# GpSimd's low parts of weights: operations of 256 columns in place of 512

## The chip, the cores and the metric

The kernel runs on one core of a Trainium2 chip. The metric is the device time of one execution in microseconds (us). The engines are TensorE (PE; PEld is its loading of weights), VectorE (DVE), ScalarE (ACT), GpSimd (POOL) and SyncE (SP, which issues nearly all the transfers). Line numbers such as L197 are those of the kernel before; the change adds four lines, so that L197 there reads L201 in the changed kernel, and L186 reads L188.

## What is computed

One inference step of a two-layer decoder trunk, for a prompt of 1024 positions and for 8 sampled sequences of 8 positions each, with one set of float32 weights. Layer 0 mixes tokens by a gated depthwise convolution beside a stick-breaking attention, layer 1 by a short gated convolution beside a causal pooling. Each mixer has an input and an output projection, and each layer ends in a SwiGLU block. Cut to what matters here:

```
def swiglu(h, w_in, w_out):
    g, u = jnp.split(h @ w_in, 2, axis=-1)
    return (jax.nn.silu(g) * u) @ w_out

    for layer in range(DEPTH):
        hn = rms_norm(h, norm_mix_g[layer])
        mix = ...            # projections hn @ w_in, token mixer, @ w_out
        h = h + mix
        h = h + swiglu(rms_norm(h, norm_ffn_g[layer]), w_ffn_in[layer], w_ffn_out[layer])
    y = rms_norm(h, norm_final_g)
```

D_MODEL is 1024 and FFN_DIM is 2816, so that nearly all of the arithmetic is products of activations with weight matrices of 1024 rows or columns.

## The kernel before, in words

**Tokens.** The 1088 columns (1024 of the prompt, 64 sampled) are worked in two groups: GA has columns 0 to 511, GB columns 512 to 1087 (576 of them, in two pieces of 288). Activations lie with channels on partitions.

**Products in three passes.** A float32 operand is split into a high part, which is the operand rounded to the format that PE multiplies (`fp32r`), and a low part, the remainder. A product is three matmuls: high weight by high activation, high by low, and low weight by high activation (`mm3`, L231 to L236; L235 is the matmul).

**Weights.** Weight blocks of 128 by 1024 values are loaded by SP into `stage` (4 buffers). `w_split` (L175) makes from each an `hl` tile (3 buffers): ACT writes the high part, POOL the low part as `stage - high`. The list `seq` fixes the order, and `w_next` (L222) hands out the next `hl` and first has the splits up to two blocks further on issued. For a **plain** block (L183 to L187) ACT writes all 1024 columns in one operation (L184), and POOL subtracts in two operations of 512 columns (L186). The weights of the output projection of the SwiGLU block are such plain blocks too.

**Forms.** Most of the SwiGLU input projections are done by a scheme with 7 products in place of 8 (`strassen`, L504; its matmuls are L511). For each pair of weight blocks, gate `sg` and up `su`, it needs sums of their halves: DVE makes them (L200, L201, L202, and L214 for the last), and `cut` (L194) splits each of the 7 halves of 512 columns: ACT writes the high part (L196), POOL the low part in one operation of 512 columns (L197). They go into four `hl` tiles, r = 0 to 3, with 2, 2, 2 and 1 halves. The 7 products use them in that order; the last product needs r = 3, which is the sum `sum_c`. DVE adds the products together from PSUM (L515), ACT applies the activation (L540), and POOL multiplies the two halves of the SwiGLU (L490); the result `hid` is split by ACT (L240) and DVE (L241).

**Order.** The kernel is scheduled by hand: every engine runs its instructions in the order in which the Python code issues them. In the SwiGLU block two `strassen` calls are followed by two output blocks (`run_ffn`, L544 to L580), in which DVE adds each result to `hb` (L295); the sums for the next `strassen` are put between these adds (L576). In `strassen`, the fourth accumulator W waits until DVE has emptied the first one. Other work of POOL lies between the low parts: squares (L252), products (L490, L465), and in layer 1 some splits of activations (L1755).

Of the kernel before, what the change touches and what calls it, by code (L numbers as in the profile page):

```python
# [12 lines left out]
OP = mybir.AluOpType  # L13
# [16 lines left out]
def f32(ap):  # L30
    return ap.bitcast(F)
# [26 lines left out]
def trunk_kernel(ctx, tc, x_prompt, x_sample, cache_k, cache_v, state_conformer, state_shortconv, state_pool,  # L58
# [4 lines left out]
    pe, act, dve, pool, sp = nc.tensor, nc.scalar, nc.vector, nc.gpsimd, nc.sync  # L63
# [97 lines left out]
    def w_load(upto):  # L161
        while nxt[0] < min(upto, len(loads)) and nxt[0] - 4 not in stage:
            i = nxt[0]
            src, kt = loads[i]
            stage[i] = wpool.tile([128, 1024], F, name="stage", bufs=4)
            sp.dma_start(stage[i].rearrange("p (k n) -> p k n", k=kt), src)
            nxt[0] += 1

    def need(upto):
        a, b, _ = seq[min(upto, len(seq)) - 1]  # L170
        return max(a, b or 0) + 1

    sums, parts_, thin = {}, [], [False]

    def w_split(upto):  # L175
        while nxt[1] < min(upto, len(seq)):
            i = nxt[1]
            a, b, r = seq[i]
            w_load(need(i + 1))
            hl = wpool.tile([128, 2, 1024], FR, name="hl", bufs=3)  # L180
            lo, hi = slice(0, 512), slice(512, 1024)
            if b is None:
                st = stage.pop(a)  # L183
                act.activation(hl[:, 0], st, AF.Copy)  # L184
                for c in (lo, hi):
                    pool.tensor_tensor(hl[:, 1, c], st[:, c], f32(hl[:, 0, c]), op=OP.subtract)  # L186
                hls[i] = hl.rearrange("p s (k n) -> p s k n", k=loads[a][1])  # L187
            else:  # L188
                sg, su = stage.get(a), stage.get(b)
                if r == 0:  # L190
                    sums["a"], sums["b"] = (sums["p"].tile([128, n], F, name=f"sum{n}") for n in (1024, 512))
                sa, sb = sums["a"], sums["b"]

                def cut(hl=hl, src=None):  # L194
                    for c, x in zip((lo, hi), src):
                        act.activation(hl[:, 0, c], x, AF.Copy)  # L196
                        pool.tensor_tensor(hl[:, 1, c], x, f32(hl[:, 0, c]), op=OP.subtract)  # L197

                if r == 0:
                    todo = [lambda: dve.tensor_tensor(sb, su[:, lo], su[:, hi], op=OP.add),  # L200
                            lambda: dve.tensor_tensor(sa[:, hi], sg[:, lo], su[:, lo], op=OP.subtract),  # L201
                            lambda cut=cut: (dve.tensor_tensor(sa[:, lo], sb, sg[:, lo], op=OP.subtract),  # L202
                                     cut(src=(sa[:, lo], sa[:, hi])))]
                    if thin[0]:
                        parts_.extend(todo)
                    else:
                        for f in todo:
                            f()
                else:
                    while parts_:  # L210
                        parts_.pop(0)()
                    if r == 2:
                        sums["c"] = sums["p"].tile([128, 512], F, name="sum_c")
                        dve.tensor_tensor(sums["c"], sg[:, hi], sa[:, lo], op=OP.subtract)  # L214
                    cut(src=(sb, sg[:, lo]) if r == 1 else (su[:, hi], sg[:, hi]) if r == 2 else (sums["c"],))
                if r == 2:
                    stage.pop(a), stage.pop(b)
                hls[i] = hl.rearrange("p s (f k n) -> p s f k n", f=2, k=4)
            nxt[1] += 1
    wj = [0]  # L220

    def w_next(live=0):  # L222
        j = wj[0]
        wj[0] += 1
        w_split(j + 3 - live)
        w_load(need(j + 6 - live))
        return hls.pop(j)
# [155 lines left out]
    def run_out(g, accs, x, gcol, ks=K0, slot=lambda: None, then=None):  # L383
        then = then or (g, x)

        def fin(n, a):
            added(g, hb[:, n, g.cs], a)
            add_squares(g, hb[:, n, g.cs], n == 0)

        a0, a1 = pair(g, accs, x, ks, {}, slot)  # L390
        fin(0, a0)
        fin(1, a1)
        for n in range(2, 6):
            slot()
            h = w_next()
            a = accs()
            block(g, a, h, x, ks, slot=slot)
            fin(n, a)
        slot()
        a0, a1 = pair(g, accs, x, K0, {k: [lambda k=k: prep(*then, k, pc(gcol + k)), lambda: low(0)]  # L400
                                       for k in range(6)}, slot)
        w_split(wj[0] + 3)
        for n, a in ((6, a0), (7, a1)):
            fin(n, a)
            prep(*then, n, pc(gcol + n))
            low(1)
        low()
# [290 lines left out]

    feed(GA, x1a, 0)
    w_split(2)  # L700
    feed(GA, x1a, 1)
    feed(GA, x1a, 2)
# [1240 lines left out]
```

## Time and profile before

| | |
|---|---|
| median of 3 runs | 2638.32 us (2637.15 to 2640.58) |
| time of the profiled execution | 2634.16 us |
| its span, first to last instruction | 2632.3 us |
| DVE busy | 1665.4 us (63%), 2330 instructions |
| ACT busy | 1109.4 us (42%), 1884 instructions |
| POOL busy | 1603.6 us (61%), 1236 instructions |
| granted TensorE clock, mean | 0.989 |

The profiled execution is one of its own and 0.16% shorter than the median of the runs. Durations come from it. A row of the groups gives a line of the kernel, the engine, the operation, `out<-in`, shapes and count, then busy time in us and the mean of one in ns, then the idle time of the engine just before, with who ended it. In a row of the waits the three numbers are us in total, times, and the longest. A row of the timeline begins with the start and the duration in us, and merges neighbours of one line (x3).

### The profile page before, as it was taken

What the parts mean: (1) busy time and instruction counts of PE and PEld (TensorE: products, weight loads), DVE (VectorE), ACT (ScalarE), POOL (GpSimd) and SP (SyncE); (2) the same over time, 40 slices, a digit from 0 to 9 for tenths busy, and PEclk for the clock granted to TensorE, in tenths of its full rate; (3) what the DMA queues carried; (4) which work ended last, traced back from release to release, by engine and by line L of the source; (5) the groups of instructions that cost most, each with busy time, mean ns of one, the idle gap of its engine ahead of it and who ended that gap; (6) DMA issues with size and microseconds to landing.
All of it is one profiled execution on the core that took longest, in us unless ns stands there. A gap on an engine that the chain in (4) does not pass through costs nothing. (4 is left out here: it accounts for less than half of the span.)

```text
span 2632.3 us, 41236 instructions
## 1 busy us (share of the span) xinstructions
PE 2529.6 (96%) x15759; PEld 2232.6 (85%) x15759; DVE 1665.4 (63%) x2330; ACT 1109.4 (42%) x1884; POOL 1603.6 (61%) x1236
## 2 busy tenths in 40 slices
PE   8989999999999999999999999999999999999998
PEld 6788877887766657999999988888888888999997
DVE  4683777868766643366666633447776778677655
ACT  5435766753443324344333431133433334443333
POOL 6756243544333328478877742256888887987775
PEclk9999999999999999999999999999999999999999
DMA  7332231234445442422323321142323332333332
GB/s 218 114 104 72 63 106 45 62 88 142 133 135 157 119 128 77 144 73 81 91 86 97 103 88 41 43 123 75 89 88 97 97 100 79 108 92 112 90 88 77
DMA packets 355484, 258.30 MB, mean 98 GB/s; under 512 B 22913, under 2 KB 303617, under 8 KB 355272
## 3 DMA queue, kind: packets, MB, share of 16 engines
q1 hardware_dynamic: 355256, 255.66, 33.1%
q8 instruction: 125, 2.05, 0.3%
q14 instruction: 71, 0.58, 0.1%
q10 hardware_dynamic: 32, 0.01, 0.0%
HBM read 237.41 MB, written 18.69 MB: 97 GB/s over the span
## 5 line engine op out<-in xcount | busy, mean ns | idle before, releaser
L186 POOL TENSOR_TENSOR hl<-stage,hl 128x512 fp32r<-128x512 f32 x464 | 633.9, 1391 | 463.5 <-ACT hl L184 319.3
L235 PE MATMUL acc<-x,hl 128*128 128x512 f32 (+1 forms) x3648 | 790.3, 353 | 14.6 <-DVE hb L295 8.8
L235 PEld LDWEIGHTS acc<-x,hl 128*128 128x128 f32 x3648 | 587.1, 191 | 100.7 <-issue 39.6
L235 PE MATMUL acc<-hid,hl 128*128 128x288 f32 (+1 forms) x3096 | 556.9, 336 | 12.8 <-DVE hb L295 5.8
L235 PEld LDWEIGHTS acc<-hid,hl 128*128 128x128 f32 x3096 | 472.2, 190 | 78.9 <-issue 11.3
L295 DVE TENSOR_TENSOR hb<-acc,hb 128x512 f32<-128x512 f32 (+1 forms) x360 | 256.7, 718 | 185.9 <-PE acc L235 184.3
L511 PE MATMUL acc<-x,hl 128*128 128x288 f32 (+1 forms) x2676 | 362.1, 290 | 5.1 <-POOL x L1755 3.1
L511 PEld LDWEIGHTS acc<-x,hl 128*128 128x128 f32 x2676 | 349.3, 188 | 6.9 <-POOL x L1755 3.3
L197 POOL TENSOR_TENSOR hl<-sum,hl 128x512 fp32r<-128x512 f32 x180 | 236.6, 1343 | 158.5 <-ACT hl L196 158.5
L515 DVE TENSOR_TENSOR tmp<-acc,tmp 128x288 f32<-128x288 f32 (+1 forms) x420 | 173.7, 441 | 229.9 <-ACT tmp L527 137.3
L184 ACT ACTIVATE hl<-stage 128x1024 fp32r<-128x1024 f32 x232 | 243.2, 1053 | 174.5 <-PE acc L235 102.0
L197 POOL TENSOR_TENSOR hl<-stage,hl 128x512 fp32r<-128x512 f32 x180 | 269.2, 1519 | 10.0 <-ACT hl L196 10.0
L511 PE MATMUL acc<-b,hl 128*128 128x256 f32 (+1 forms) x1548 | 215.7, 290 | 11.9 <-DVE tmp L515 10.2
L235 PE MATMUL acc<-x1t,hl 128*128 128x288 f32 x1152 | 216.6, 296 | 4.4 <-POOL hl L186 4.4
L511 PEld LDWEIGHTS acc<-b,hl 128*128 128x128 f32 x1548 | 201.9, 189 | 17.1 <-ACT hl L196 11.8
L235 PEld LDWEIGHTS acc<-x1t,hl 128*128 128x128 f32 x1152 | 196.0, 188 | 22.6 <-POOL hl L186 4.9
L196 ACT ACTIVATE hl<-sum 128x512 fp32r<-128x512 f32 x180 | 103.1, 623 | 233.1 <-DVE sum L202 211.0
L291 DVE TENSOR_TENSOR tmp<-acc,rr 128x512 f32<-128x512 f32 (+1 forms) x108 | 75.3, 710 | 152.0 <-PE acc L235 147.2
L252 POOL TENSOR_TENSOR ss<-ss,tmp 128x512 f32<-128x512 f32 (+1 forms) x69 | 107.8, 1563 | 75.2 <-ACT tmp L251 72.4
L196 ACT ACTIVATE hl<-stage 128x512 fp32r<-128x512 f32 x180 | 105.6, 618 | 68.5 <-PE acc L235 63.3
L490 POOL TENSOR_TENSOR tmp<-tmp 128x576 f32<-128x576 f32 (+1 forms) x85 | 127.2, 1496 | 9.3 <-ACT tmp L467 8.3
L241 DVE TENSOR_TENSOR hid<-tmp,hid 128x512 fp32r<-128x512 f32 (+1 forms) x88 | 100.0, 1138 | 47.2 <-ACT hid L240 47.1
(288 smaller groups left out, 3312.4 us busy)
## 6 DMA issues: line engine op xcount, KB each, us to landing
stage<-in_w_ffn_in_dram SPq DMA_DIRECT2D x176, 512.0 KB
stage<-in_w_ffn_out_dram SPq DMA_DIRECT2D x88, 512.0 KB
stage<-in_w_in_even_dram SPq DMA_DIRECT2D x40, 512.0 KB
kst<-in_cache_k_dram SPq DMA_DIRECT2D x64, 256.0 KB
vst<-in_cache_v_dram SPq DMA_DIRECT2D x64, 256.0 KB
stage<-in_w_out_even_dram SPq DMA_DIRECT2D x16, 512.0 KB
stage<-in_w_in_odd_dram SPq DMA_DIRECT2D x16, 512.0 KB
stage<-in_w_out_odd_dram SPq DMA_DIRECT2D x16, 512.0 KB
```

What stands on the lines that cost most here:

```text
L184: act.activation(hl[:, 0], st, AF.Copy)
L186: pool.tensor_tensor(hl[:, 1, c], st[:, c], f32(hl[:, 0, c]), op=OP.subtract)
L196: act.activation(hl[:, 0, c], x, AF.Copy)
L197: pool.tensor_tensor(hl[:, 1, c], x, f32(hl[:, 0, c]), op=OP.subtract)
L235: pe.matmul(acc[:, b, :c1 - c0], w, xs[:, xi, c0 - o:c1 - o], start=first and s == 0, stop=last and s == 2)
L241: dve.tensor_tensor(dst[:, 1], src, f32(dst[:, 0]), op=OP.subtract)
L252: pool.tensor_tensor(ss[:, g.cs], ss[:, g.cs], t[:, :g.n], op=OP.add)
L291: dve.tensor_tensor(d, a, r, op=OP.mult)
L295: dve.tensor_tensor(d, a, d, op=OP.add)
L490: (dve if both and f == NF - 1 else pool).tensor_tensor(t[:, :n], t[:, :n], u[:, :n], op=OP.mult)
L511: pe.matmul(acc[:, :w2], h[:, wi, i, k], xk[:, xi], start=k == 0 and s == 0, stop=k == 3 and s == 2)
L515: dve.tensor_tensor(out, acc[:, :w2], x, op=OP.add)
```

## The change

In both places of `w_split` where POOL writes a low part, its operation of 512 columns becomes two of 256 columns each. ACT's operations, DVE's, the matmuls and the transfers stay as they were, and so does each engine's order of work.

```
+    LOW = 256
...
             if b is None:
                 st = stage.pop(a)
                 act.activation(hl[:, 0], st, AF.Copy)
-                for c in (lo, hi):
+                for c0 in range(0, 1024, LOW):
+                    c = slice(c0, c0 + LOW)
                     pool.tensor_tensor(hl[:, 1, c], st[:, c], f32(hl[:, 0, c]), op=OP.subtract)
...
                 def cut(hl=hl, src=None):
                     for c, x in zip((lo, hi), src):
                         act.activation(hl[:, 0, c], x, AF.Copy)
-                        pool.tensor_tensor(hl[:, 1, c], x, f32(hl[:, 0, c]), op=OP.subtract)
+                        for c0 in range(0, 512, LOW):
+                            s = slice(c0, c0 + LOW)
+                            pool.tensor_tensor(hl[:, 1, c][:, s], x[:, s], f32(hl[:, 0, c][:, s]), op=OP.subtract)
```

This is how POOL's program reads in the SwiGLU block of layer 1, group GA, before: the low parts of one `strassen` (four `hl` tiles, 20001 to 20122) and the beginning of the next. A row gives the line, the operation, its tiles and columns, and the semaphores that it waits for.

```order
L490 TENSOR_TENSOR tmp_19945<-tmp_19945,tmp_19943 128x512 [waits Activation_49,Pool_49]
L197 TENSOR_TENSOR hl_20001<-sum1024_20002,hl_20001 128x512 [waits Activation_49] x2
L197 TENSOR_TENSOR hl_20046<-sum512_20003,hl_20046 128x512 [waits Activation_49]
L197 TENSOR_TENSOR hl_20046<-stage_19915,hl_20046 128x512 [waits DMAHW4_49,Activation_49]
L197 TENSOR_TENSOR hl_20088<-stage_19917,hl_20088 128x512 [waits DMAHW5_49,Activation_49]
L197 TENSOR_TENSOR hl_20088<-stage_19915,hl_20088 128x512 [waits Activation_49]
L197 TENSOR_TENSOR hl_20122<-sum_c_20089,hl_20122 128x512 [waits Activation_49]
L197 TENSOR_TENSOR hl_20154<-sum1024_20155,hl_20154 128x512 [waits PE_49,Activation_49]
```

The same place in the changed kernel, where the first tile is hl_20614 and the tile of `sum_c` hl_20741 (up to there):

```order
L201 TENSOR_TENSOR hl_20661<-sum512_20616,hl_20661 128x256 [waits Activation_49]
L201 TENSOR_TENSOR hl_20661<-sum512_20616,hl_20661 128x256
L201 TENSOR_TENSOR hl_20661<-stage_20524,hl_20661 128x256 [waits DMAHW4_49,Activation_49]
L201 TENSOR_TENSOR hl_20661<-stage_20524,hl_20661 128x256
L201 TENSOR_TENSOR hl_20705<-stage_20526,hl_20705 128x256 [waits DMAHW5_49,Activation_49]
L201 TENSOR_TENSOR hl_20705<-stage_20526,hl_20705 128x256
L201 TENSOR_TENSOR hl_20705<-stage_20524,hl_20705 128x256 [waits Activation_49]
L201 TENSOR_TENSOR hl_20705<-stage_20524,hl_20705 128x256
L201 TENSOR_TENSOR hl_20741<-sum_c_20706,hl_20741 128x256 [waits Activation_49]
L201 TENSOR_TENSOR hl_20741<-sum_c_20706,hl_20741 128x256
```

Each operation has become two in the same place; the first carries the waits and the second none.

On PE, these are the first matmuls of that `strassen` before; each `x3` is the three matmuls of one 128-column slice of the weights.

```order
L511 MATMUL acc_20087<-x1_0_71,hl_20001 128x256 [waits DVE_49,Activation_49]
L511 MATMUL acc_20087<-x1_0_71,hl_20001 128x256
L511 MATMUL acc_20087<-x1_0_71,hl_20001 128x256 [waits Pool_49]
L511 MATMUL acc_20087<-x1_1_72,hl_20001 128x256 x3
L511 MATMUL acc_20087<-x1_2_73,hl_20001 128x256 x3
L511 MATMUL acc_20087<-x1_3_74,hl_20001 128x256 x3
L511 MATMUL acc_20087<-x1_4_75,hl_20001 128x256 [waits Activation_49]
```

And in the changed kernel:

```order
L515 MATMUL acc_20704<-x1_0_71,hl_20614 128x256 [waits DVE_49,Activation_49]
L515 MATMUL acc_20704<-x1_0_71,hl_20614 128x256
L515 MATMUL acc_20704<-x1_0_71,hl_20614 128x256 [waits Pool_49]
L515 MATMUL acc_20704<-x1_1_72,hl_20614 128x256 x3
L515 MATMUL acc_20704<-x1_2_73,hl_20614 128x256 x2
L515 MATMUL acc_20704<-x1_2_73,hl_20614 128x256 [waits Pool_49]
L515 MATMUL acc_20704<-x1_3_74,hl_20614 128x256 x3
L515 MATMUL acc_20704<-x1_4_75,hl_20614 128x256 [waits Activation_49]
```

PE now waits for a low part twice per 512 columns: at its first slice for the first operation of POOL, and at its third slice for the second.

On ACT, the high parts of the same tiles before:

```order
L196 ACTIVATE hl_20088<-stage_19915 128x512
L240 ACTIVATE hid_19875<-tmp_19945 128x512 [waits Pool_49]
L196 ACTIVATE hl_20122<-sum_c_20089 128x512 [waits DVE_49,PE_49,Pool_49]
L527 ACTIVATE tmp_20149<-acc_20121 128x256 [waits PE_49]
L196 ACTIVATE hl_20154<-sum1024_20155 128x512 [waits DVE_49,Pool_49]
L196 ACTIVATE hl_20154<-sum1024_20155 128x512
L196 ACTIVATE hl_20193<-sum512_20156 128x512 [waits PE_49,Pool_49]
```

And in the changed kernel:

```order
L198 ACTIVATE hl_20705<-stage_20524 128x512
L244 ACTIVATE hid_20481<-tmp_20554 128x512 [waits Pool_49]
L198 ACTIVATE hl_20741<-sum_c_20706 128x512 [waits PE_49,DVE_49,Activation_49,Pool_49]
L531 ACTIVATE tmp_20769<-acc_20740 128x256 [waits PE_49]
L198 ACTIVATE hl_20774<-sum1024_20775 128x512 [waits DVE_49,Activation_49,Pool_49]
L198 ACTIVATE hl_20774<-sum1024_20775 128x512
L198 ACTIVATE hl_20815<-sum512_20776 128x512 [waits PE_49,Activation_49,Pool_49]
```

Some of ACT's operations now also wait for an earlier one of ACT itself; their order is the same.

More of the change, by code (lines that the diff above doesn't have):

```diff
@@ L171, in need @@
         return max(a, b or 0) + 1
+    LOW = 256
     sums, parts_, thin = {}, [], [False]
@@ L184, in w_split @@
                 act.activation(hl[:, 0], st, AF.Copy)
-                for c in (lo, hi):
+                for c0 in range(0, 1024, LOW):
+                    c = slice(c0, c0 + LOW)
                     pool.tensor_tensor(hl[:, 1, c], st[:, c], f32(hl[:, 0, c]), op=OP.subtract)
@@ L196, in cut @@
                         act.activation(hl[:, 0, c], x, AF.Copy)
-                        pool.tensor_tensor(hl[:, 1, c], x, f32(hl[:, 0, c]), op=OP.subtract)
+                        for c0 in range(0, 512, LOW):
+                            s = slice(c0, c0 + LOW)
+                            pool.tensor_tensor(hl[:, 1, c][:, s], x[:, s], f32(hl[:, 0, c][:, s]), op=OP.subtract)
                 if r == 0:
```

## The prediction

> **What bounds the kernel now.** I read the page first, then who waits for whom on PE, then the table by stretches, then the timeline of one stretch.
>
> ```profile
> span 2632.3 us, 41236 instructions
> PE 2529.6 (96%) x15759; PEld 2232.6 (85%) x15759; DVE 1665.4 (63%) x2330; ACT 1109.4 (42%) x1884; POOL 1603.6 (61%) x1236
> ...
> L186 POOL TENSOR_TENSOR hl<-stage,hl 128x512 fp32r<-128x512 f32 x464 | 633.9, 1391 | 463.5 <-ACT hl L184 319.3
> ...
> L197 POOL TENSOR_TENSOR hl<-sum,hl 128x512 fp32r<-128x512 f32 x180 | 236.6, 1343 | 158.5 <-ACT hl L196 158.5
> ...
> L197 POOL TENSOR_TENSOR hl<-stage,hl 128x512 fp32r<-128x512 f32 x180 | 269.2, 1519 | 10.0 <-ACT hl L196 10.0
> ```
> ```profile
> L197 POOL TENSOR_TENSOR hl<-sum_c,hl 128x512 fp32r<-128x512 f32 x60 | 89.6, 1493 | 1.4 <-ACT hl L196 1.4
> ```
>
> PE is busy 96% of the span, so over the whole kernel PE sets the pace. The change touches 464 + 180 + 180 + 60 = 884 operations of POOL, which make up 1229 of its 1604 us. It can move the end only where PE waits. These are the waits that POOL, or a DVE held up by POOL, may end:
>
> ```profile
> PE acc L235 <- DVE hb L295: 14.6, 10, 5.2
> PE acc L511 <- DVE tmp L515: 11.9, 14, 2.8
> PE acc L235 <- POOL hl L186: 9.0, 7, 2.8
> ...
> PE acc L511 <- POOL x L1755: 3.1, 1, 3.1
> ...
> PE acc L511 <- POOL hl L197: 1.6, 4, 0.5
> ```
>
> That is 40.2 us in all. How close POOL is to PE differs by stage:
>
> ```profile
> 2062.34:2094.87 32.53, 31.83 (x217) 28.83 (x216) 22.89 (x33) 12.94 (x22) 27.40 (x20) 1.00 0.32 97
> 2494.26:2529.38 35.12, 35.12 (x266) 35.12 (x265) 21.77 (x32) 13.31 (x22) 27.29 (x21) 1.00 0.32 91
> ```
> ```profile
> 1835.00:1895.00 60.00, 55.75 (x415) 53.15 (x416) 40.37 (x58) 29.20 (x49) 55.83 (x40) 0.97 0.33 94
> 2220.00:2271.00 51.00, 47.90 (x361) 47.66 (x360) 38.58 (x48) 22.32 (x40) 48.11 (x34) 1.00 0.31 94
> 2271.00:2340.00 69.00, 68.02 (x504) 66.74 (x503) 45.23 (x60) 31.58 (x53) 64.10 (x47) 1.00 0.26 77
> ```
>
> The columns are PE, PEld, DVE, ACT and POOL. The first row is one pair of strassens with its two output blocks in group GA, the second such a pair in GB. In GB PE has no idle time and POOL has 7.8 us to spare; in GA POOL has 5.1. The last three are the beginnings of these stages in layer 1: POOL has 4.2, 2.9 and 4.9 us left there. This is the GA pair:
>
> ```profile
> 2065.12 3.81 POOL L197 TENSOR_TENSOR hl<-sum,hl 128x512 fp32r<-128x512 f32 x3 [3.17 <-ACT hl L196]
> 2068.88 4.71 POOL L197 TENSOR_TENSOR hl<-stage,hl 128x512 fp32r<-128x512 f32 x3
> 2073.55 1.74 POOL L197 TENSOR_TENSOR hl<-sum_c,hl 128x512 fp32r<-128x512 f32 x1
> 2077.24 4.25 POOL L197 TENSOR_TENSOR hl<-sum,hl 128x512 fp32r<-128x512 f32 x3 [1.95 <-ACT hl L196]
> ...
> 2086.45 1.30 POOL L197 TENSOR_TENSOR hl<-sum_c,hl 128x512 fp32r<-128x512 f32 x1
> 2087.70 5.06 POOL L186 TENSOR_TENSOR hl<-stage,hl 128x512 fp32r<-128x512 f32 x4
> ```
> ```profile
> 2068.88 1.85 DVE L214 TENSOR_TENSOR sum_c<-stage,sum 128x512 f32<-128x512 f32 x1
> 2070.65 1.78 DVE L241 TENSOR_TENSOR hid<-tmp,hid 128x512 fp32r<-128x512 f32 x1
> 2072.36 1.78 DVE L200 TENSOR_TENSOR sum<-stage 128x512 f32<-128x512 f32 x1
> 2074.06 1.78 DVE L201 TENSOR_TENSOR sum<-stage 128x512 f32<-128x512 f32 x1
> 2075.76 0.68 DVE L202 TENSOR_TENSOR sum<-sum,stage 128x512 f32<-128x512 f32 x1
> 2076.36 2.39 DVE L515 TENSOR_TENSOR tmp<-acc,tmp 128x256 f32<-128x256 f32 x6
> ```
> ```profile
> 2077.38 1.67 PE L511 MATMUL acc<-b,hl 128*128 128x256 f32 x12 [0.66 <-DVE tmp L515]
> ```
>
> DVE's sums take 1.78 us while POOL works and 0.68 when POOL is idle. They start 1.70 apart, and so do POOL's operations (4.71 + 1.74 us for four): the two engines take turns, one operation each. That goes even for an operation of five columns:
>
> ```profile
> 1857.19 1.22 DVE L266 TENSOR_TENSOR nw<-nw 128x5 f32<-128x5 f32 x1
> 1858.44 1.22 DVE L267 TENSOR_SCALAR nw<-nw 128x5 f32<-128x5 f32 x1
> ```
>
> So an operation of POOL is the unit for which DVE waits, and the change halves it. DVE's operations with an input in PSUM aren't held: six of L515 take 2.39 us beside a busy POOL. [...]
>
> **The price of a half.** No low part of 256 columns is in this trace. The nearest rows are subtractions and sums of other tiles:
>
> ```profile
> L901 POOL TENSOR_TENSOR hb<-hb,rr 128x512 f32<-128x512 f32 x4 | 5.1, 1288 | 0.0
> ...
> L1861 POOL TENSOR_TENSOR ss<-ss,tmp 128x256 f32<-128x256 f32 x6 | 4.4, 738 | 7.1 <-ACT tmp L1860 7.0
> ```
>
> 512 columns take 1.29 us, 256 take 0.74, so a fixed 0.19 us is paid per operation. Neighbours overlap a little: four low parts in 5.06 us (row at 2087.70) start (5.06 - 1.29) / 3 = 1.257 apart, 0.03 to 0.04 less than one lasts. Two halves then cost 2 x (0.74 - 0.04) = 1.40 against 1.26: **+0.14 us for each of the 884**, 124 us of POOL's time. The ends: +0 (the fixed part overlaps altogether) and 2 x 0.738 - 1.257 = +0.22 (no overlap).
>
> [...]
>
> **Part by part.**
>
> *GB pairs, layer 0's too, and background stages*: +0. 18 of a pair's operations are low parts: 18 x 0.14 = 2.5 us, and POOL has 7.8 to spare.
>
> *GA pairs.* POOL's first stretch (2065.12 to 2075.29) has 7 low parts and three that DVE broke into for 1.70 - 1.26 = 0.44 us each. Now it lasts 7 x 0.14 = 1.0 longer, and 0.4 to 0.9 more since DVE gets in at more seams. DVE's chain gets shorter by about 0.55 for each of four held operations, 2 us, so that PE's 0.66 at 2077.38 goes, and the second stretch no longer waits 1.95 for L202. What is late next is POOL itself: it begins the second stretch at about 2077.1 in place of 2077.24 and needs another 1.0 us up to the output block. There PE gets by with less than before: the last product needs only the first half of `sum_c` (-0.55), the output block three quarters of its tile (3 x 0.70 in place of 2 x 1.26, -0.4). PE arrives 1.0 - 0.15 - 0.55 = 0.3 late, or 0.4 at the output block. I take **+0.3 for each of nine pairs, +2.7**.
>
> *The beginnings.* Of the 40, 34 and 47 operations of POOL in the three stretches 33, 25 and 36 are low parts (the same view for L186 and L197 alone): 4.6 + 3.5 + 5.0 = 13.1 us more for POOL, which has 12.0 left. Most of that idle time lies ahead of waits for L202 and is of use only up to there; halves that come 0.55 earlier give back some. I take +5, and +2 for two stretches of the same kind (around 1030 and 1225): **+7**.
>
> *Relief of DVE outside the pairs.* An example:
>
> ```profile
> 438.11 3.39 DVE L953 TENSOR_TENSOR kt<-kall,kt 64x512 fp32r<-64x512 f32 x2
> ```
> ```profile
> 442.37 1.19 PE L235 MATMUL acc<-x,hl 128*128 128x512 f32 x2 [5.22 <-DVE hb L295]
> ```
>
> Two held operations in front of L295: 2 x 0.55 = 1.1 us of the 5.2 go. A quarter of the 14.6 us behind L295 is 3.7. Of the 11.9 behind L515 the pairs account for some 5.5; of the rest 2.5 go, the five-column operations foremost. With about 1 us in small waits: **-7**.
>
> *PE waits for POOL*: 9.0 us in 7 waits, each up to 0.55 earlier if the first half is what PE wants, less where DVE gets into the seams: **-2.5**.
>
> *More waits.* PE's added waits follow operations that ended earlier in all but these places; the GB pair, where PE waits for POOL at every half tile and is never idle, prices them at 0. ACT's added wait for itself: the groups of three high parts below have three waits in the third of the first, two in the third of the second.
>
> ```profile
> 2064.41 1.68 ACT L196 ACTIVATE hl<-sum 128x512 fp32r<-128x512 f32 x3 [6.03 <-DVE sum L202]
> ...
> 2076.53 1.67 ACT L196 ACTIVATE hl<-sum 128x512 fp32r<-128x512 f32 x3 [2.23 <-DVE sum L202]
> ```
>
> 1.68 against 1.67: 0, at most 0.01 x 146 such operations. Stage buffers come free 0.14 to 0.3 us later; loads are issued blocks ahead.
>
> **Sum**: 2.7 + 7 - 7 - 2.5 = +0.2 on the profiled execution's 2634.16 us. The median of the runs is 2638.32, so I forecast **2638.5**: no change. A measurement of this kernel can tell about 0.2%, 5 us, from none.
>
> **Rivals.**
>
> *Relief wins (faster).* If DVE's waits are worth half of the 26.5 us behind L295 and L515, and POOL's fixed part half overlaps (+0.07): -13 - 2.5 + 5 = -10, 2628. For it: DVE runs L200 at 1.78 for 0.68 throughout. Against: in the GA pair POOL takes up at once what DVE yields.
>
> *POOL becomes the bound (slower).* The place is the GA pair and the beginnings, the price the fixed part of the second half. At +0.22 a pair's 14 low parts up to the output block cost another 14 x 0.08 = 1.1 us, and POOL's 1.95 us of idle time are gone: nine pairs +13, the beginnings +11, relief -9.5: +14, 2652. It decides from about +0.17 per operation. For it: POOL at 27.4 of 32.5 and 64.1 of 69. Against: the overlap of neighbours.
>
> *The halves don't free DVE*: if two neighbours of POOL pass as one, only the fixed part is left: +10 to +13, 2649. Against it: at 2068.88 to 2075.29 DVE gets in between any two neighbours.
>
> **How the numbers follow.** No change 0.46, relief 0.28, POOL bound 0.22, not freed 0.04. Faster by over 0.2%: 0.28; within: 0.46; slower: 0.26. The range takes in the likeliest parts of the cases at both sides, 2623 to 2653.
>
> **What would show it.** Of the changed kernel: low parts of 256 columns 0.70 apart; L200 to L202 about 1.15 apart where they alternated at 1.70; in the GA pair no wait of PE for L515, but one for POOL ahead of the last product, and no idle time of POOL in front of the second stretch; pairs of 32.8 us in GA and 35.1 in GB. I'd be wrong if halves cost as much as 0.74 each, or if the pair in GA got shorter than 32.3.

## The result, and the profile after

The change makes the kernel slower: 2678.43 us median (2677.12 to 2680.93, 4 runs) against 2637.74 us beside it, a ratio of 1.0152 with a 95% interval of 1.0137 to 1.0167, some 40 us. The forecast of 2638.5 and its range up to 2653 missed it. The lines below are the page of the changed kernel, then who waits for whom on PE.

```profile
span 2676.2 us, 42377 instructions
PE 2540.8 (95%) x15759; PEld 2239.2 (84%) x15759; DVE 1607.8 (60%) x2330; ACT 1110.2 (41%) x1884; POOL 1775.8 (66%) x2120
L188 POOL TENSOR_TENSOR hl<-stage,hl 128x256 fp32r<-128x256 f32 x928 | 729.0, 819 | 431.6 <-ACT hl L185 294.9
L201 POOL TENSOR_TENSOR hl<-sum,hl 128x256 fp32r<-128x256 f32 x360 | 268.4, 779 | 109.7 <-ACT hl L198 108.0
L201 POOL TENSOR_TENSOR hl<-stage,hl 128x256 fp32r<-128x256 f32 x360 | 318.0, 913 | 8.7 <-ACT hl L198 8.7
```
```profile
PE acc L239 <- DVE hb L299: 29.5, 18, 4.1
PE acc L515 <- POOL hl L201: 10.9, 17, 0.8
PE acc L239 <- POOL hl L188: 9.3, 15, 2.8
...
PE acc L515 <- DVE tmp L519: 6.7, 4, 3.7
PE acc L515 <- POOL x L1759: 6.4, 1, 6.4
```

POOL is busy 172 us longer, DVE 58 us shorter, and PE waits twice as long as before for DVE's additions to `hb` (29.5 us, 14.6 before), although DVE has less to do. The next rows are the same pair of GA as in the prediction, a pair of GB, and two stretches of layer 1: the beginning of GB, and the end of GA.

```profile
2083.05:2117.76 34.71, 32.37 (x216) 28.84 (x217) 22.82 (x33) 13.04 (x22) 30.33 (x38) 1.00 0.31 91
2538.01:2573.13 35.12, 35.12 (x266) 35.12 (x265) 20.36 (x32) 13.21 (x22) 31.28 (x39) 1.00 0.30 91
2251.43:2308.82 57.39, 50.48 (x361) 50.05 (x359) 35.10 (x49) 22.49 (x40) 52.15 (x59) 0.94 0.31 89
2218.53:2251.43 32.90, 27.10 (x128) 22.29 (x127) 29.00 (x39) 11.37 (x22) 15.13 (x18) 0.95 0.27 78
```

GB pairs are unchanged. The GA pair takes 2.2 us more, and this is what DVE and POOL do at its end (the changed kernel's timeline, DVE first):

```profile
2112.33 0.69 DVE L299 TENSOR_TENSOR hb<-acc,hb 128x512 f32<-128x512 f32 x1 [1.41 <-PE acc L239]
2112.93 4.08 DVE L204 TENSOR_TENSOR sum<-stage 128x512 f32<-128x512 f32 x1
2116.94 0.68 DVE L299 TENSOR_TENSOR hb<-acc,hb 128x512 f32<-128x512 f32 x1
```
```profile
2108.22 1.42 POOL L201 TENSOR_TENSOR hl<-sum_c,hl 128x256 fp32r<-128x256 f32 x2
2109.59 5.62 POOL L188 TENSOR_TENSOR hl<-stage,hl 128x256 fp32r<-128x256 f32 x8
2115.14 1.32 POOL L494 TENSOR_TENSOR tmp<-tmp 128x512 f32<-128x512 f32 x1
2120.84 1.44 POOL L201 TENSOR_TENSOR hl<-sum,hl 128x256 fp32r<-128x256 f32 x2 [4.38 <-ACT hl L198]
```

The sum L204 takes 4.08 us; alone such a sum takes 0.67 to 0.68 (L205, of the same shape, 0.67 at 2117.54 beside an idle POOL). It asks at 2112.93; POOL passes three seams (a seam is where one operation of POOL ends and the next begins) between its halves and one to L494, and DVE is let in at none of them: it runs its 0.68 us from about 2116.3 on, when POOL's last operation ends. PE then waits for L299, which is queued behind the sum, and POOL itself stands idle for 4.38 us, since its next low part needs the sums that follow L204. I call this a **long hold** (over 1.5 us more than the operation takes). By count over one trace of each, the kernel before has none, the changed one 12, 47 us of holding together: eleven L204 and this product of DVE at the end of GA.

```profile
2216.15 6.86 DVE L494 TENSOR_TENSOR tmp<-tmp 128x512 f32<-128x512 f32 x1 [0.70 <-ACT tmp L544]
```

### The profile page after: what moved, and what is told of

Same layout as the page of the kernel before. It is cut to its first block, busy times and chain, and to the rows that moved or that the text cites. A ratio compares the mean times of both kernels' runs of the same rounds, so it can differ in the third digit from the quotient of the medians.

```text
span 2676.2 us, 42377 instructions
## 1 busy us (share of the span) xinstructions
PE 2540.8 (95%) x15759; PEld 2239.2 (84%) x15759; DVE 1607.8 (60%) x2330; ACT 1110.2 (41%) x1884; POOL 1775.8 (66%) x2120
## 5 line engine op out<-in xcount | busy, mean ns | idle before, releaser
L188 POOL TENSOR_TENSOR hl<-stage,hl 128x256 fp32r<-128x256 f32 x928 | 729.0, 819 | 431.6 <-ACT hl L185 294.9
L299 DVE TENSOR_TENSOR hb<-acc,hb 128x512 f32<-128x512 f32 (+1 forms) x360 | 257.0, 719 | 206.0 <-PE acc L239 203.9
L515 PE MATMUL acc<-x,hl 128*128 128x288 f32 (+1 forms) x2676 | 368.8, 292 | 9.9 <-POOL x L1759 6.4
L519 DVE TENSOR_TENSOR tmp<-acc,tmp 128x288 f32<-128x288 f32 (+1 forms) x420 | 174.4, 442 | 283.6 <-ACT tmp L531 156.0
L201 POOL TENSOR_TENSOR hl<-sum,hl 128x256 fp32r<-128x256 f32 x360 | 268.4, 779 | 109.7 <-ACT hl L198 108.0
L201 POOL TENSOR_TENSOR hl<-stage,hl 128x256 fp32r<-128x256 f32 x360 | 318.0, 913 | 8.7 <-ACT hl L198 8.7
L494 POOL TENSOR_TENSOR tmp<-tmp 128x576 f32<-128x576 f32 (+1 forms) x85 | 124.5, 1465 | 10.6 <-ACT tmp L471 9.9
L239 PE MATMUL acc<-x1a,hl 128*128 128x512 f32 x480 | 122.0, 408 | 2.9 <-POOL hl L188 1.5
```

Source lines behind the costliest of these rows:

```text
L201: pool.tensor_tensor(hl[:, 1, c][:, s], x[:, s], f32(hl[:, 0, c][:, s]), op=OP.subtract)
L239: pe.matmul(acc[:, b, :c1 - c0], w, xs[:, xi, c0 - o:c1 - o], start=first and s == 0, stop=last and s == 2)
L299: dve.tensor_tensor(d, a, d, op=OP.add)
L494: (dve if both and f == NF - 1 else pool).tensor_tensor(t[:, :n], t[:, :n], u[:, :n], op=OP.mult)
L515: pe.matmul(acc[:, :w2], h[:, wi, i, k], xk[:, xi], start=k == 0 and s == 0, stop=k == 3 and s == 2)
L519: dve.tensor_tensor(out, acc[:, :w2], x, op=OP.add)
```

## The experiments

Two theories at first. **Lockout**: the holds are the loss. **Price** (a rival of the prediction): POOL's added time makes POOL the bound. Four kernels:

```
e1_plain512   -  for c0 in range(0, 1024, LOW): c = slice(c0, c0 + LOW)      # plain blocks
              +  for c0 in range(0, 1024, 512): c = slice(c0, c0 + 512)
e2_forms512   -  for c0 in range(0, 512, LOW): s = slice(c0, c0 + LOW)       # forms
              +  for c0 in range(0, 512, 512): s = slice(c0, c0 + 512)
e3_sum_later  +  dve.memset(sb[:, :128], 0.0)          # ahead of L204
e4_price_only    (before, 512 columns, and behind each low part)
              +  pool.tensor_tensor(hl[:, 1, e], x[:, 508:], f32(hl[:, 0, e]), op=OP.subtract)   # e: last 4 columns
```

> Plain blocks are back at 512 columns, only the forms stay at 256. Lockout theory (the loss is a dozen DVE operations, eleven sums L204 and one product, that miss a seam in a train of plain 256-column pieces and are then held 3.3 to 6.2 us until POOL is idle, 47 us in all): no DVE operation is held for more than 1.3 us, the time is 2638 to 2650. Price theory (0.135 us more of POOL's time per low part makes POOL the bound; 420 of the 884 keep it): about half the loss stays, 2655 to 2662.

> Forms are back at 512, only the plain blocks stay at 256. Lockout theory: the trains of plain pieces are there still, so L204 is still held for 3 us or more in most GA pairs (at least 6 times in all) unless it comes at another moment; 2660 to 2676. Price theory: 464 of 884 prices stay, and those lie mostly outside the pairs' tight stretches: 2648 to 2658.

> All low parts in 256 columns as in the change; ahead of each first sum L204 DVE writes 128 columns of zeros into the tile that the sum then overwrites, so that the sum comes about 0.3 us later. Lockout theory: L204 came 0.07 to 0.2 us ahead of the end of a piece; 0.3 us later it comes at the beginning of the next piece, waits under 0.6 us and is let in at the next seam: at least eight of the eleven long holds go and the time falls by 25 us or more, to 2636 to 2653, though DVE has more to do. Price theory: POOL's work is unchanged and DVE's grows: 2678 to 2684.

> Low parts of 512 columns as before the change, each followed by a POOL subtraction of its last 4 columns again, which costs about the fixed part of an operation (0.15 to 0.2 us; 884 times, 130 to 175 us of POOL's time, as much as the change or more). Lockout theory: no train of 256-column pieces, no hold above 1.5 us; the price alone gives 2640 to 2652. Price theory: POOL's time is that of the change, so is the result: 2672 to 2690.

| kernel | ratio to before (95%) | median us | long holds, us | POOL busy us |
|---|---|---|---|---|
| e1 plain 512, forms 256 | 1.0108 (1.0084 to 1.0132) | 2666.83 | 13, 36 | 1677.3 |
| e2 plain 256, forms 512 | 1.0070 (1.0049 to 1.0092) | 2654.63 | 8, 27 | 1700.7 |
| e3 sum later | 1.0200 (1.0177 to 1.0223) | 2689.39 | 26, 80 | 1766.7 |
| e4 price only | 1.0194 (1.0175 to 1.0213) | 2689.50 | 0, 0 | 1821.7 |

None of the four times is the one that the lockout theory gave; of its holds only e2's and e4's came out as it said. e1 still has holds, while plain operations of 512 columns run. e3 moved the sum and got more holds, in GB too: the moment of arrival isn't what decides. And e4 is 51 us slower with no hold at all, so POOL's time has a price of its own. The price theory had the times of e2 and e4, and missed e1 and e3 by some 5 us each. Price alone doesn't do either: e1 adds 74 us of POOL's time and loses 30 us, e2 adds 97 and loses 17.

But e4 isn't the change's price alone. Its additional operation writes columns that POOL has just written, and waits for that: POOL is idle for 0.08 us ahead of each of the 884. So its low parts start 1.52 us apart in place of 1.26, about twice the price of the change, and its runs are never long without a stop. POOL's rows, and an L204 that came behind 16 operations of POOL, counted through these stops:

```profile
2118.03 1.29 POOL L199 TENSOR_TENSOR hl<-stage,hl 128x512 fp32r<-128x512 f32 x1
2119.40 0.20 POOL L201 TENSOR_TENSOR hl<-stage,hl 128x4 fp32r<-128x4 f32 x1
2119.55 1.28 POOL L199 TENSOR_TENSOR hl<-stage,hl 128x512 fp32r<-128x512 f32 x1
```
```profile
2129.37 0.88 DVE L204 TENSOR_TENSOR sum<-stage 128x512 f32<-128x512 f32 x1
```

31 operations of DVE came like this one behind 13 to 17 operations of POOL, and none was held for long. In e2 two GA pairs differ by the hold alone (windows, then DVE's rows in the second):

```profile
2079.52:2111.77 32.25, 31.61 (x217) 29.02 (x216) 22.79 (x33) 12.96 (x22) 28.93 (x25) 1.00 0.33 99
2144.02:2177.47 33.45, 31.77 (x217) 28.86 (x216) 23.98 (x32) 12.96 (x22) 28.83 (x25) 1.00 0.36 105
```
```profile
2172.27 0.69 DVE L299 TENSOR_TENSOR hb<-acc,hb 128x512 f32<-128x512 f32 x1 [0.97 <-PE acc L239]
2172.87 3.85 DVE L204 TENSOR_TENSOR sum<-stage 128x512 f32<-128x512 f32 x1
```

POOL works as long in both; the held pair is 1.2 us longer. So both act, and the question is what makes a hold. In all these runs no operation that came within 9 us of POOL's last idle time, or of the last time it let DVE in, was held long, and that suggested a third theory: how long POOL has run unbroken. One kernel (m1, executed once, as m2 and m3 below) measures it by itself; two try to break the runs with a small addition of DVE:

```
e5_let_in (after), e6_before_let_in (before), in strassen:
             add(U[:, b], X[:, 1], U[:, a])
+            dve.tensor_tensor(G_[:, w2:w2 + 4], U[:, 0:4], G_[:, 0:4], op=OP.add)
```

> The kernel's own work is left out. 96 trials: POOL runs an unbroken train of 35 subtractions of 256 columns, or 20 of 512, and DVE asks for one addition of 512 columns (two inputs in SBUF) t = 1 to 18.8 us after the train's start, in three phases each; 18 of the trials have an addition of 4 columns let in about 6 us ahead of it. Theory of the unbroken run (POOL lets DVE in at the next seam only while it has stopped within the last 10 us, be it idle or for DVE): up to t = 9 every addition is let in at the first or second seam (hold up to 0.7 us at 256, 1.3 at 512, or one piece more); from t = 11 on most are held to the end of the train, 5 us and more, at both widths; with the small addition 6 us ahead all are let in at once. Theory of the moment (it is the distance to the seam at arrival that decides, and short pieces make it likely): long holds at any t in one of the three phases, few at 512, and the small addition changes nothing.

> All low parts in 256 columns as in the change; in each strassen DVE does one more addition, of 4 columns from two SBUF tiles (its result is overwritten), some 6 us ahead of L204, so that POOL's run is broken there. If the long holds are the whole loss: none is left, 2637 to 2645. If holds and price share it (in the group GA pairs a held pair takes 34.70, the one pair without a hold 33.26, before 32.5): GA pairs of about 33.2, the product and the sums behind 2190 not held, 2650 to 2662. If the price alone is the loss: 2676 to 2684. By the theory of the moment the holds stay or come at random.

> The kernel before, low parts of 512 columns, with the same small addition. Before, L200 missed one seam in most GA pairs (1.17 us, 10 to 12 us after POOL's last stop). If those misses cost PE something: 2630 to 2636. If not, or if the additions cost as much: 2637 to 2641.

m1: at 256 columns all additions that came up to 8.8 us after the start were let in within 1.3 us, and of those at 9.0 us and later one was; the other 22 were held for 6.3 to 15.4 us, to the end of the train. At 512 columns the limit lay at 16 us. Both are about 13 operations. That the run's length decides is confirmed; that it is time isn't. The small addition was let in, but at 256 all nine additions behind it were still held (at 512 none came later than the limit). So e5 kept its holds (16, 62 us) and its time: 2683.19, ratio 1.0159 (1.0131 to 1.0187). e6 gave 2638.36, 0.9996 (0.9981 to 1.0010): nothing. Its profile shows that operations of 512 columns aren't safe either: six long holds, 18 us, behind 7 to 10 operations, four of them in GA pairs like this one. That execution was the slowest of e6's 12 (2647.46 us); whether the others had holds isn't known.

```profile
2070.10 3.11 DVE L200 TENSOR_TENSOR sum<-stage 128x512 f32<-128x512 f32 x1
```

Next, the count against the time at other widths, a break of 256 columns in place of 4, and the opposite direction:

```
e7_full_break (after):
+            dve.tensor_tensor(G_[:, b], U[:, a], G_[:, a], op=OP.add)
e8_plain1024 (before):
-                for c in (lo, hi):
-                    pool.tensor_tensor(hl[:, 1, c], st[:, c], f32(hl[:, 0, c]), op=OP.subtract)
+                pool.tensor_tensor(hl[:, 1], st, f32(hl[:, 0]), op=OP.subtract)
```

> The kernel's own work is left out; trains of POOL as in the run with the 96 trials, now also of 128 and 384 columns, and with breaks of 4 to 512 columns. There additions were let in at the next seam up to 8.8 us after the start of a train of 256-column operations (0.695 us apart), and up to 15.7 us at 512 (1.257 apart): 13 operations each. Theory of the count (each operation without a pause of POOL closes the seam a little, and after 13 it is shut): shut from about 5.5 us on at 128 columns (if those are 0.42 apart), from 9.0 at 256, from 12.7 at 384, from 16.2 at 512. Theory of the time: the limit at 128 lies near 9 us as at 256, and 384 between 9 and 16 only by chance. Breaks: an addition of 4 columns 6 us ahead does not open the seam again, one of 512 columns does; 128 and 256 lie between.

> All low parts in 256 columns as in the change; in each strassen DVE does one more addition of 256 columns (288 in GB) from two SBUF tiles, 6 us ahead of L204; its result is overwritten. If such a break opens the seams again, L204 is let in at the next seam; the long holds go, and what is left over the kernel before is the price of the halves alone: GA pairs of 33.0 to 33.4, 2650 to 2664. If the holds cost nothing beside the price: as the change, 2676 to 2684. If a break of 256 columns is too short, the holds stay and the time too.

> The other direction: the low part of a plain block in one operation of 1024 columns, forms in 512 as before. 232 operations fewer, so some 35 us less of POOL's time, 2 operations fewer in a GA pair's run; but DVE and PE wait up to 2.36 us for one. Price and count: POOL is later nowhere, no hold: 2630 to 2640. If the length of one operation decides (relief theory turned round: longer waits of DVE): 2642 to 2655.

m2: without a break the first addition held came at 5.3 us for 128 columns, 9.8 for 256, 12.5 for 384 and 13.8 for 512, where others were let in up to 16.95. In operations of POOL that is the 12th to the 15th: at all four widths every addition that came during the 11th or earlier was let in, and every one during the 15th or later was held. The count decides, not the time. The breaks came out at 35 columns (the first at 20); 30 of 36 additions behind them stayed shut out (a later expectation says 27, a slip in counting).

e7: the holds are gone but one (an L245 at 1044.85, 6.30 us), and 16 us with them: 2662.23, ratio 1.0083 (1.0059 to 1.0107), though DVE and POOL are both busier than in the change. DVE's break and sum, and the GA pair and the end of GA as windows:

```profile
2100.58 0.97 DVE L536 TENSOR_TENSOR tmp<-tmp 128x256 f32<-128x256 f32 x1
...
2107.38 0.73 DVE L204 TENSOR_TENSOR sum<-stage 128x512 f32<-128x512 f32 x1
```
```profile
2077.36:2110.77 33.41, 32.06 (x217) 28.96 (x216) 22.36 (x35) 13.04 (x22) 32.03 (x39) 1.00 0.33 95
2208.94:2236.24 27.30, 25.29 (x127) 21.15 (x126) 25.66 (x38) 10.33 (x21) 17.35 (x19) 1.00 0.33 97
```

e8 is no gain: 2649.28, 1.0038 (1.0026 to 1.0051), inside what was expected if the length of one operation decides. GA pairs get 0.3 us shorter, but by count over its trace 52 operations of DVE wait 1.6 to 2.2 us for one of 1024 columns, none of them in a GA pair.

Last, breaks of the right lengths, and what the breaks of e7 cost by themselves:

```
e9_before_full_break (before):
+            dve.tensor_tensor(G_[:, b], U[:, a], G_[:, a], op=OP.add)
```

> The kernel's own work is left out; 90 trials with trains of 35 operations of 256 columns. In the run before, all the breaks came out at 35 columns, and 27 of 36 additions behind them stayed shut out; the lengths are now 4, 64, 128, 256 and 512 columns. Theory of the count with a break that puts POOL back in step if it lasts: 4 and 64 columns leave the addition at 11 to 14.5 us shut out for 9 us and more, 512 lets all 9 in at the next seam, 256 most of them. If any break counted as a stop, all would be let in; if only idle time of POOL counts, none would. The last 9 trials stop POOL for an ACT operation after its ninth: then all are let in by each theory but that of the time since the train's start. Without a break the seam shuts between 9.0 and 9.8 us.

> The kernel before, low parts of 512 columns, with the same breaks as the run with the full break: what the breaks cost by themselves. That run took 2662.2, the change 2678.4, the kernel before about 2638. If the breaks cost little (0 to 6 us): 2638 to 2644, the halves alone cost about 20 us, and the long holds the other 16 to 20. If the breaks cost 10 us or more (2648 and above), the halves alone cost 14 or less, and the holds 26 or more.

m3: two trials without a break, 0.24 us apart in arrival; a row of L114 is POOL's train of 35, and L122 the addition.

```profile
239.18 24.38 POOL L114 TENSOR_TENSOR low<-st,hi 128x256 fp32r<-128x256 f32 x35
...
264.54 23.94 POOL L114 TENSOR_TENSOR low<-st,hi 128x256 fp32r<-128x256 f32 x35
```
```profile
247.96 0.70 DVE L122 TENSOR_TENSOR o<-a 128x512 f32<-128x512 f32 x1
...
273.56 15.47 DVE L122 TENSOR_TENSOR o<-a 128x512 f32<-128x512 f32 x1
```

The first came 8.78 us after the train's start, the second 9.02. All ten that came during the 11th to the 13th operation were let in, two of eight during the 14th, none of 18 later. Behind a break of 4 columns 0 of 9 were let in, behind 64, 128, 256 and 512 columns all 36, and all 9 where POOL had stopped for an ACT operation (0.32 us idle) after its ninth. The rows of two breaks, L118, 6 us after the start, and of the additions behind them:

```profile
921.97 0.33 DVE L118 TENSOR_TENSOR o<-a 128x4 f32<-128x4 f32 x1
927.10 13.47 DVE L122 TENSOR_TENSOR o<-a 128x512 f32<-128x512 f32 x1
...
1147.32 0.39 DVE L118 TENSOR_TENSOR o<-a 128x64 f32<-128x64 f32 x1
1152.52 1.13 DVE L122 TENSOR_TENSOR o<-a 128x512 f32<-128x512 f32 x1
```

I had expected 64 columns to be too short, and they weren't.

e9: the breaks alone cost 2642.38, ratio 1.0016 (1.0003 to 1.0030), without a hold. The halves beside them cost 1.0083 - 1.0016 = 0.67%, some 18 us, of which the L245 held at 1044 takes about 6 (PE starts 9.4 us later there than before, with e9 2.2). That leaves about 12 us for the halves alone, and **some 28 of the 40 us for the holds**, where 16 to 20 had been expected. By the intervals of the two ratios this is uncertain by some 7 us, and it takes for granted that the breaks cost the same beside halves as beside whole operations.

A similar split comes out of the changed kernel's own trace: followed matmul by matmul against the kernel before, PE falls behind by some 8 us at the two holds of layer 0's beginning (1219 and 1258), by 12 in the GA pairs, seven of them held (16.6 in all nine, less 0.5 each, which is what the halves cost from e9 to e7), by 3.0 at the end of GA (32.90 us against 29.95; against e7, which has 27.30 without the hold, it is 5.6) and by about 2 at the hold of 2341: 25 to 28 us of the 43.9 that the two spans differ by.

## Why the prediction was wrong

**The step that failed** is the sentence against the rival "the halves don't free DVE": that DVE gets in between any two neighbours of POOL. It was read from a stretch in which POOL had just begun. DVE does get in there (1.78 us a sum), but in the trains, after some 13 operations without a break, POOL's seams were shut (in m3 0.70 us for an addition that came at 8.78 us, 15.47 for one at 9.02), and halves reach that count in half the columns: 9 us in place of 16. By count over the trace of before, at most 10 or 11 operations lie between the last break and the moment when DVE asks; in the changed kernel it is 15 to 17 at the held sums of GA. So before stood close to a cliff, and no row of its trace showed a long hold. The rival had 0.04, and its price of 10 to 13 us was the fixed part alone; a hold that lasts until POOL is idle had no place in the sum, and it cost some 28 of the 40 us. The other 12 lie, as far as the runs tell, in terms that were too small: the beginnings and PE's waits for POOL, below.

*Who is held*: of the prediction's two rows of five columns L266 has two inputs in SBUF, L267 a single one. L267 took 1.22 us while POOL worked, 0.17 in the eleven places where POOL was idle, so it was held as well. L263, also with a single input in SBUF, took 0.18 at 1856.63 while POOL worked. What decides it for a single input was not tried, and no term of the sum needs it.

*The price of a half*: right. Eight halves in a row take 5.62 us, (5.62 - 0.73) / 7 = 0.70 apart, and the sums where the engines alternate start 1.15 apart (2091.99, 2093.14, 2094.28):

```profile
2091.99 1.23 DVE L204 TENSOR_TENSOR sum<-stage 128x512 f32<-128x512 f32 x1
2093.14 1.22 DVE L205 TENSOR_TENSOR sum<-stage 128x512 f32<-128x512 f32 x1
2094.28 1.22 DVE L206 TENSOR_TENSOR sum<-sum,stage 128x512 f32<-128x512 f32 x1
```

+0.14 us for each of 884 it is, 124 us; m2's trains of 128, 256, 384 and 512 columns (0.41, 0.68, 0.95 and 1.22 us apart without DVE) give a fixed part of 0.14 too. POOL's busy time grew by more, 172 us; it also counts the time for which DVE's operations hold POOL's (in the kernel before a low part takes 1.74 us at 2073.55, where DVE takes turns with POOL, and 1.30 at 2086.45), and the two weren't separated.

*GB pairs*: right, 35.12 before and after.

*GA pairs*: the halves' own +0.3 was about right (33.41 with breaks against 32.88 for the kernel before with breaks: +0.5), and so were the signs: POOL has no idle time ahead of its second stretch, and PE waits for POOL once in the forms and not for L519 (it also waits for POOL once, 0.2 us, at the output block). The pair came out at 34.71 for the hold that wasn't in it: L299 is queued behind it. The rows are the changed kernel's POOL, its PE waits from 2083 to 2118, and the pair of e9, before with breaks:

```profile
2096.76 1.43 POOL L201 TENSOR_TENSOR hl<-sum_c,hl 128x256 fp32r<-128x256 f32 x2
2098.15 4.67 POOL L201 TENSOR_TENSOR hl<-sum,hl 128x256 fp32r<-128x256 f32 x6
```
```profile
PE acc L239 <- DVE hb L299: 2.5, 2, 1.3
PE acc L515 <- POOL hl L201: 0.8, 1, 0.8
PE acc L239 <- POOL hl L188: 0.2, 1, 0.2
```
```profile
2066.28:2099.16 32.88, 31.83 (x218) 28.87 (x216) 24.07 (x36) 12.95 (x22) 28.15 (x20) 1.00 0.32 94
```

*The beginnings*: the mechanism right, the size not. +5 for three stretches was forecast; the second alone (50.96 to 57.39, no hold in it) cost 6.4, the first 3.2 (59.85 to 63.05), the third 4.9 with its hold. In the second PE waits 6.4 us in place of 3.1 for `x`, which POOL splits behind low parts, and runs at a granted clock of 0.94 in place of 1.00, and the same 361 matmuls keep it busy 2.6 us longer (50.48 us, 47.90 before). Whether the halves bring that clock is open: e9, with whole operations, has 0.94 in this stretch too (2224 to 2279 there, PE busy 50.81 us). I had set POOL's idle time against the price as if it could be moved.

*Relief of DVE*: right in e7, where nearly no hold covers it: PE's waits for L299 are 12.6 us (14.6 before) and for L519 5.8 (11.9), 8 us in all (7 forecast). The rows are PE's waits in e7:

```profile
PE acc L515 <- POOL hl L201: 15.9, 25, 1.2
PE acc L239 <- DVE hb L299: 12.6, 7, 4.1
...
PE acc L239 <- POOL hl L188: 9.2, 15, 2.8
...
PE acc L515 <- DVE tmp L519: 5.8, 3, 3.5
```

The GA pair of e4 would fit: POOL is as busy as in e7's (31.93 and 32.03 us), but DVE waits for whole operations, and the pair takes 34.72 in place of 33.41 us. It doesn't show the relief, since POOL also stands idle there for 18 x 0.08 = 1.4 us ahead of the additional operations.

```profile
2098.05:2132.77 34.72, 32.78 (x217) 29.38 (x216) 21.37 (x33) 13.06 (x22) 31.93 (x39) 1.00 0.32 92
```

*PE's waits for POOL*: wrong. 9.0 us for plain blocks stayed 9.3 (-2.5 forecast); for forms 1.6 became 10.9.

*More waits*: nothing speaks against the 0; no run tried them apart.

*POOL becomes the bound* (0.22, 2652): by mechanism the second half of the truth. e7, without the holds, has POOL busy 32.03 of 33.41 us in the pair, and 2662.

## What to carry to other kernels

Cutting an operation of GpSimd in two doesn't only cost its fixed part (0.14 us here) and shorten a wait (a sum took 1.22 us in place of 1.78): it doubles the number of operations in an unbroken run, and in the trains here a VectorE operation with two SBUF inputs was let in only within the first 13 or so. e4 doubles the number as well and has no hold: there GpSimd stops for 0.08 us ahead of every second operation, and it was 51 us slower all the same. Where both engines matter, count GpSimd's operations between two of its stops (or between two VectorE operations of 64 columns or more that get in), not only its microseconds. A stretch in which two engines take turns (1.22 us for a sum at 2093.14) says nothing about one where the first has run alone for long (4.08 at 2112.93).

## What the runs showed of the hardware that had not been expected

- In the trains, POOL's unbroken run shut DVE out after 11 to 14 operations, at 128, 256, 384 and 512 columns alike: 15.47 us for an addition that came 9.02 us after the start of a train, 0.70 for one that came 8.78 after it. The hold lasted until POOL was idle (in m3 from 273.56 to 289.03, with POOL's train ending at 288.48); at 128 columns DVE was let in one to four operations earlier. In the 15.47 us DVE waited for 21 operations that all started after it had asked.
- In m3 the seam opened again where POOL was idle for 0.32 us, or where DVE worked for 64 columns or more (0.39 us with its wait for 64), not for 4 (0.33 us). In e4, with idle times of 0.08 us, none of the 31 operations of DVE behind 13 to 17 of POOL was held; whether it is these stops or the 4 columns of every second operation was not tried apart.
- In the kernels the limit isn't as sharp as in the trains. Counted from the last 0.1 us of idle POOL or the last operation of DVE that got in, holds came after 7 to 18 operations, and the fewest, 7 to 10, were e6's, where the same counts gave no hold in the kernel before. In the changed kernel 18 operations of DVE that came after 13 or more were let in; for 11 of them POOL had stopped for less than 0.1 us on the way (0.01 us at 1294.7, ahead of the L204 at 1297.27). What inside POOL closes the seam was not tried, and stays open.
- With the same 15759 matmuls PE is busy 11.2 us longer in the changed kernel (2540.8 and 2529.6). 2.6 us of it lie at 2251 to 2308, where the granted clock is 0.94 in place of 1.00; what set the clock there was not tried.
